# The seam between two transformer layers: which PSUM pool stays open, which engine rounds, and in which banks the row maxima stand

## The chip, the cores and the metric

The kernel runs on one core of one Trainium2 chip. The metric is the device time of the whole kernel in microseconds (us), the median of three runs. The core has five engines, each with its own queue in which instructions are taken in order: TensorE (PE, matmuls, its weight loads shown as PEld), VectorE (DVE), ScalarE (ACT), GpSimd (POOL) and SyncE (SP, which here issues most of the DMA transfers). Matmul results land in PSUM, eight banks of 512 fp32 words in each of 128 partitions; everything else on the chip stands in SBUF.

## The reference

The reference computes two layers of a diffusion backbone over 512 latent tokens and 256 context tokens, all with 1024 channels. Cut to what matters here:

```
for l in range(2):
    h   = rmsnorm(x) * (1 + scale) + shift          # "n1", modulated by the conditioning vector
    u   = h @ w_in                                  # one combined projection
    a   = glu -> depthwise conv(31) -> layernorm -> silu -> projection       # conv mixer
    b   = bidirectional mLSTM, 4 heads of 256 (gates: log_sigmoid, running sums and maxima), times o-gate
    c   = attention, 8 query heads and 2 key heads of 64, QK norm, axial rotary
    x  += gate * ((sigmoid(g_i) * (a, b, c)) @ w_out)
    x  += gate2 * ffn(modulated rmsnorm(x))         # gated, width-3 depthwise conv before the activation
```

Context tokens use the same weights with their own modulation, and read context tokens only. The output is the latent stream, so the second layer needs no context rows after its keys and values.

## The kernel before

**Layout.** Activations stand with channels on the partitions: eight tiles `xs[m]` of 128 channels by 768 positions, 512 latent (the segment X) and 256 context (XC). Layer 0 computes both, in PSUM tiles of 768 columns; layer 1 works on the latent positions, with the context only for keys and values.

**Precision.** Products are made from fp32 values that are split in a rounded high part and a low part. Every weight block of 128 x 128 thus gives three matmuls in `accumulate` (L717): high times high, and the two mixed products. The activations of a norm are `hh` and `hl`, the weights `wh` and `wl`.

**Weights.** All weights come through one stream in units of four blocks. SP loads a unit into `raw`; `Weights.split` lets ScalarE make `wh` (L215) and GpSimd `wl` (L217). In two kinds of stage the flag `W.shared` is set: where the merged mixers are projected, and in layer 0's last projection for the context half. There VectorE makes `wl` for odd units. A unit is split SPLITS units ahead of use.

**Order of the work.** TensorE's order is written out by hand. A `Filler` holds a queue of projections; `fill.step()` issues one k-step of the projection at the head and then a tick to all "chains", generators in which `yield n` means "go on after n ticks". Chains carry what VectorE, ScalarE and GpSimd do, and the small matmuls among it. `fill.settle()` ticks until all chains have ended, without further projection steps.

**PSUM.** Four banks are the small pools `sm` and `pv`, two buffers each. The other four are the pool `mm` for projections: `open_banks(l)` makes two buffers of 1024 words in layer 0, and four of 512 in layer 1. At the end of layer 0 `layer.close()` (L1752) closes the one and `open_banks(1)` (L783) opens the other; the new one can be written when the last reader of the old one is done.

**The boundary between the layers.** Layer 0's last projection, "down", runs once for the latent positions and once for the context positions, 256 columns wide, with 8 output tiles m. When tile m is complete, VectorE adds it to the residual stream (`residual`, L1619), ScalarE squares the result (`Norm.square`, L637), VectorE adds the square to a running sum (L639), and SP stores the tile. Beside the context half runs the chain `norm.apply` for the latent half of layer 1's first norm: for each of 8 k, VectorE multiplies by the reciprocal root (L679), ScalarE scales and shifts (L680), VectorE rounds to `hh` (L687), and VectorE, for k = 2 and 4 GpSimd, makes `hl` (L372). The context half of the norm follows as a chain in layer 1.

**First stage of a layer.** `opt["first"]` gives the order of the first projections: in layer 0 the gates and q, k, Q, K abreast ("G"), then v of head 0; in layer 1 "Q g K v". When the gate projection is complete, its evacuation starts the chain `mgates`: exponentials, a logarithm, two running scans and small differences on 36 rows, and at the end the matmuls L904 and L906 that spread the result. Between its parts stand ticks, `yield 5, 1, 2, 1, 2, 2, 2, 1, 3, 2`, 21 in all. All projections but the last are drained, then the chains are settled, then the last projection follows.

**Heads of the mLSTM.** `HEADS` and `HEADS1` (layer 1) give for each head the projections that fill TensorE ("c" conv, "o0 o1" the output gate, "q v" the next head's) and the positions, counted in steps, at which the mLSTM's own parts are issued: D (decays), S (scores, and the denominators' sums L1131 behind them), R (row sum of the denominators, matmul L584 in `normalise`, then transfers that spread it) and V (product with v). `score_gap` is the number of ticks between two score pairs. There are two groups, 0 and 1, in each head of layer 1.

**Attention.** `prepare(i)` finds the row maxima of head i: a matmul of each block of 128 queries with 512 keys into a `pv` bank (L1472), reduced by VectorE (L1473); the same with 256 context keys, two query blocks to a bank (L1479, L1481); then a transposition `rp` (L1489) in `pv`. Between them stand ticks. The attention products use `pv` too (L1565), read by L1573. Beside them run the gate projections for the merge in `mm`, evacuated by L369.

Of the kernel before, what the change touches and what calls it, by code (L numbers as in the profile page):

```python
# [17 lines left out]
D = 1024  # L18
# [33 lines left out]
HEADS1 = [["c o0 o1 q v", "2:S0 4:D1 16:R0 22:S1 39:R1 40:V0 61:V1 61:D*"]] * 3 +     [["c o0 o1 b b x0", "2:S0 4:D1 15:R0 21:S1 35:R1 38:V0 51:V1 51:s"]]  # L52
# [3 lines left out]
    score_gap=5, rows_gap=4, mask_gap=2, prep=2)  # L56
OPT = [dict(COMMON, partial=2, heads=HEADS, early=1, first_max=5, send_gap=2, norm_gap=8, first="G v",
# [3 lines left out]
       dict(COMMON, partial=3, heads=HEADS1, early=1, first_max=8, send_gap=3, norm_gap=11, first="Q g K v",  # L61
# [126 lines left out]
class Weights:  # L188


    def __init__(self, nc, dram, l, pool, more):
        self.next, self.shared, self.more = None, False, more
# [27 lines left out]
    def take(self, *specs):  # L220
# [4 lines left out]
        if j <= 1 < j + len(specs):  # L225
            self.split(u + SPLITS + 1)
# [61 lines left out]
def build(tc, A):  # L288
# [3 lines left out]
    with ExitStack() as es:  # L292
# [327 lines left out]
        class Norm:  # L620


            def __init__(self, l, nw, sc0, sh0, opt):
# [5 lines left out]
                self.hs = []  # L629

            def square(self, k, x, seg):
# [6 lines left out]
                if k < KC - 1:  # L638
                    dve.tensor_tensor(out=self.acc[:, o:o + n], in0=self.acc[:, o:o + n], in1=q[:, o:o + n], op=ALU.add)  # L639
# [35 lines left out]
            def raw_block(self, xs, seg, k, r=None):  # L675
                o, n, s = seg
                y = t3()[:, o:o + n]
                if r is not None:
                    dve.tensor_tensor(out=y, in0=xs[k][:, o:o + n], in1=r[:, 0:n], op=ALU.mult)  # L679
                act.activation(out=y, in_=xs[k][:, o:o + n] if r is None else y, func=AF.Identity,  # L680
                               scale=self.amul[:, k, s:s + 1], bias=mods[self.l][:, self.sh0 + k, s:s + 1])
                return y

            def block_parts(self, y, seg, k):
                o, n, s = seg
                hh, hl = self.hs[k]
                dve.tensor_copy(hh[:, o:o + n], y)  # L687
                lo_part(hl[:, o:o + n], y, hh[:, o:o + n], dve if k in self.opt["dve_lo"] else pool)
# [9 lines left out]
            def apply(self, xs, seg, n, each):  # L698
# [9 lines left out]
                for k in range(KC):  # L708
                    yield each
                    y, y0 = self.raw_block(xs, seg, k + 1, r) if k < KC - 1 else None, y  # L710
                    self.block_parts(y0, seg, k)
# [1059 lines left out]
```

## Time and profile before

| | |
|---|---|
| median of 3 runs | 3040.97 us (3040.7 to 3048.51) |
| profiled execution, its own time | 3040.4 us |
| span of the profiled execution | 3038.6 us |
| TensorE busy | 2827.8 us, 93% of the span |
| VectorE busy | 1817.7 us, 60% |
| ScalarE busy | 1156.8 us, 38% |
| GpSimd busy | 1146.6 us, 38% |

The span runs from the first to the last instruction that the profiler recorded; the execution's own time holds what lies around it too. Busy times of an engine are sums over its instructions, and overlap between engines. In the rows below, a wait "A <- B" is idle time of A's engine that ended when B's instruction gave its signal. The granted clock (PEclk) is the share of full speed that TensorE was given in a stretch; it has two levels, 1.2 and 2.4 GHz, so that 0.75 means half of the stretch at each.

### The profile page before, as it was taken

What the parts mean: (1) busy time and instruction counts of PE and PEld (TensorE: products, weight loads), DVE (VectorE), ACT (ScalarE), POOL (GpSimd) and SP (SyncE); (2) the same over time, 40 slices, a digit from 0 to 9 for tenths busy, and PEclk for the clock granted to TensorE, in tenths of its full rate; (3) what the DMA queues carried; (4) which work ended last, traced back from release to release, by engine and by line L of the source; (5) the groups of instructions that cost most, each with busy time, mean ns of one, the idle gap of its engine ahead of it and who ended that gap; (6) DMA issues with size and microseconds to landing.
All of it is one profiled execution on the core that took longest, in us unless ns stands there. A gap on an engine that the chain in (4) does not pass through costs nothing. (4 is left out here: it accounts for less than half of the span.)

```text
span 3038.6 us, 42068 instructions
## 1 busy us (share of the span) xinstructions
PE 2827.8 (93%) x15970; PEld 2381.7 (78%) x15970; DVE 1817.7 (60%) x2521; ACT 1156.8 (38%) x2122; POOL 1146.6 (38%) x931
## 2 busy tenths in 40 slices
PE   7999999899889998999999988999889889899999
PEld 4888888787667887888888867887767567778887
DVE  4376787825554336876765555777774763554444
ACT  5224334324345334322322253433444344443333
POOL 2233343224244334333333333333344345444444
PEclk9999999999999999999999999999999999999999
DMA  6454334221010242333333232333322112423333
GB/s 242 133 149 69 58 67 68 49 60 52 28 28 29 63 130 93 115 101 118 118 115 115 75 102 68 65 75 67 65 75 69 39 38 76 154 87 100 93 96 110
DMA packets 156681, 262.47 MB, mean 86 GB/s; under 512 B 17784, under 2 KB 37624, under 8 KB 156480
## 3 DMA queue, kind: packets, MB, share of 16 engines
q1 hardware_dynamic: 142560, 249.67, 28.0%
q10 hardware_dynamic: 13920, 10.12, 3.1%
q8 instruction: 126, 2.06, 0.3%
q14 instruction: 75, 0.61, 0.1%
HBM read 247.05 MB, written 5.46 MB: 83 GB/s over the span
## 5 line engine op out<-in xcount | busy, mean ns | idle before, releaser
L217 POOL TENSOR_TENSOR wl<-raw,wh 128x512 fp32r<-128x512 f32 x659 | 904.6, 1379 | 1507.6 <-ACT wh L215 1461.0
L717 PE MATMUL mm<-hh,wh 128*128 128x512 f32 (+1 forms) x2672 | 963.6, 361 | 17.0 <-DVE big L1619 7.1
L717 PE MATMUL mm<-hh,wl 128*128 128x512 f32 (+1 forms) x2672 | 949.1, 355 | 10.7 <-POOL wl L217 10.6
L717 PE MATMUL mm<-hl,wh 128*128 128x512 f32 (+1 forms) x2672 | 954.4, 357 | 2.1 <-POOL hl L372 1.2
L215 ACT ACTIVATE wh<-raw 128x512 fp32r<-128x512 f32 x662 | 411.2, 625 | 580.2 <-PE mm L717 358.4
L717 PEld LDWEIGHTS mm<-hh,wh 128*128 128x128 f32 x2672 | 512.4, 192 | 113.3 <-issue 29.6
L717 PEld LDWEIGHTS mm<-hh,wl 128*128 128x128 f32 x2672 | 510.4, 191 | 89.4 <-POOL wl L217 15.5
L717 PEld LDWEIGHTS mm<-hl,wh 128*128 128x128 f32 x2672 | 512.3, 192 | 71.4 <-POOL hl L372 1.8
L717 PE MATMUL mm<-C,wh 128*128 128x512 f32 (+1 forms) x1168 | 410.2, 351 | 0.3 <-DVE C L372 0.3
L717 PE MATMUL mm<-B,wh 128*128 128x512 f32 (+1 forms) x976 | 344.4, 353 | 24.4 <-DVE big L1619 11.8
L717 PE MATMUL mm<-B,wl 128*128 128x512 f32 (+1 forms) x976 | 342.5, 351 | 9.2 <-POOL wl L217 8.8
L993 DVE SCALAR_TENSOR_TENSOR AC<-G,par,AC 128x783 f32<-128x783 f32 (+1 forms) x240 | 261.1, 1088 | 3.6
L717 PEld LDWEIGHTS mm<-C,wh 128*128 128x128 f32 x1168 | 226.6, 194 | 28.3 <-DVE C L372 0.5
L717 PEld LDWEIGHTS mm<-B,wh 128*128 128x128 f32 x976 | 190.1, 195 | 53.7 <-ACT wh L215 14.5
L717 PEld LDWEIGHTS mm<-B,wl 128*128 128x128 f32 x976 | 189.4, 194 | 37.4 <-POOL wl L217 14.2
L1669 DVE SCALAR_TENSOR_TENSOR AC<-mm,par,AC 128x511 f32<-128x511 f32 (+1 forms) x132 | 86.7, 656 | 199.0 <-ACT AC L1667 199.0
L1619 DVE SCALAR_TENSOR_TENSOR big<-mm,mod,big 128x512 f32<-128x512 f32 (+1 forms) x144 | 91.1, 657 | 116.3 <-PE mm L717 116.1
L1667 ACT ACTIVATE AC<-mm,par 128x768 f32<-128x768 f32 (+1 forms) x88 | 77.4, 880 | 145.0 <-PE mm L717 144.8
L372 POOL TENSOR_TENSOR P<-t,P 128x512 fp32r<-128x512 f32 (+1 forms) x64 | 75.1, 1175 | 139.2 <-ACT t L1550 111.2
L527 DVE SCALAR_TENSOR_TENSOR P<-C,cs,P 128x512 f32<-128x512 f32 x112 | 116.5, 1072 | 0.9 <-DMA C<-aw 0.9
L1565 PE MATMUL pv<-P,B 128*128 128x512 f32 (+1 forms) x336 | 94.6, 387 | 12.1 <-DVE G L1573 5.2
L1097 ACT ACTIVATE C<-rb,bias 128x128 f32<-128x128 f32 x312 | 96.4, 390 | 21.4 <-DMA rb<-rows 11.2
(282 smaller groups left out, 3726.5 us busy)
## 6 DMA issues: line engine op xcount, KB each, us to landing
raw<-ws SPq DMA_DIRECT2D x662, 256.0 KB, 2.6
C<-aw SPq DMA_DIRECT2D x104, 256.0 KB, 3.0
big<-aw SPq DMA_DIRECT2D x64, 256.0 KB, 4.7
P<-ws SPq DMA_DIRECT2D x30, 256.0 KB, 2.9
big<-xt SPq DMA_DIRECT2D x16, 384.0 KB, 6.3
rb<-rows ACTq DMA_DIRECT2D x40, 128.0 KB, 4.2
den<-rd ACTq DMA_DIRECT2D x40, 64.0 KB, 6.3
den<-rd SPq DMA_DIRECT2D x40, 64.0 KB, 6.3
```

What stands on the lines that cost most here:

```text
L215: self.nc.scalar.activation(out=hi, in_=raw, func=AF.Copy)
L217: eng.tensor_tensor(out=lo, in0=raw, in1=hi.bitcast(F32), op=ALU.subtract)
L372: (eng or dve).tensor_tensor(out=out, in0=src, in1=hi.bitcast(F32), op=ALU.subtract)
L527: dve.scalar_tensor_tensor(out=a_, in0=r_, scalar=cs[:, k, q:q + 1], in1=a_, op0=ALU.mult, op1=ALU.add)
L717: pe.matmul(ps[:, o:o + n], w[w_], h[h_][:, so:so + n], start=(k == 0 and i == 0 and o % 512 == 0), stop=(k == n_k - 1 and i == 2), skip_g ...
L993: dve.scalar_tensor_tensor(out=a, in0=t[:, j:j + cw], scalar=par(l, "cw", w0 + j), in1=a, op0=ALU.mult, op1=ALU.add)
L1097: act.activation(out=t[:, off + x * 128:off + x * 128 + 128], in_=rb[:, c0:c0 + 128], func=AF.Exp, bias=bcol(dr, h, key, qb))
L1565: pe.matmul(o_[:, 0:n_q], vblock(b, a_)[:, 64 * v_:64 * v_ + 128], b_[:, 0:n_q], start=(ki == 0 and x == 0), stop=(last and x == 2))
L1619: dve.scalar_tensor_tensor(out=xs[m][:, o:o + n], in0=ps[:, po:po + n], scalar=gain[:, m, s:s + 1], in1=xs[m][:, o:o + n], op0=ALU.mult, o ...
L1667: act.activation(out=t[:, 0:tq], in_=ps[:, 0:tq], func=AF.Identity, scale=fw(1), bias=fb)
L1669: dve.scalar_tensor_tensor(out=t[:, o + 1:o + n], in0=ps[:, o:o + n - 1], scalar=fw(0), in1=t[:, o + 1:o + n], op0=ALU.mult, op1=ALU.add)
```

## The change

It has seven parts.

1. The pool of layer 0 is no longer closed at layer 0's end. It stays open through layer 1's first projections, and is exchanged for the four buffers of 512 just before the first head.
2. `Norm` has a form `fold`, used for layer 1's first norm. VectorE multiplies by the reciprocal root and by the scale in one instruction. For k = 0, 1, 3, 5, 6, 7 ScalarE adds the shift and rounds to `hh` in one, and VectorE makes `hl` as (y + shift) − hh in one. For k = 2 and 4 ScalarE adds the shift, VectorE casts and GpSimd makes `hl`. For the context half, the running sums of squares are added by GpSimd.
3. While `shared` is set, weights are split one unit further ahead, and the parts of odd units go to tiles of the pool AC (`room`).
4. The ticks of `mgates` become 6, 2, 3, 2, 3, 3, 3, 2, 2, 4, 3, 33 in all, in both layers; the transfer of the row values stands alone between two of them.
5. Layer 1's first stage becomes "Q g K o v": the first half of head 0's output gate moves there from head 0.
6. In layer 1's heads the positions of R, S, V shift by some steps, and `score_gap` goes from 5 to 4.
7. The maxima over a latent block's keys go to `mm` tiles: in layer 0 two query blocks x 512 keys or four x 256 to a buffer of 1024, in layer 1 as many to a tile as before. The context queries' maxima and `rp` stay in `pv`.

The diff, without the rows that pass `room` on:

```diff
-HEADS1 = [["c o0 o1 q v", "2:S0 4:D1 16:R0 22:S1 39:R1 40:V0 61:V1 61:D*"]] * 3 +     [["c o0 o1 b b x0", "2:S0 4:D1 15:R0 21:S1 35:R1 38:V0 51:V1 51:s"]]
+HEADS1 = [["c o1 q v", "2:S0 4:D1 18:R0 25:S1 41:R1 42:V0 60:V1 60:D*"]] + [["c o0 o1 q v", "2:S0 4:D1 18:R0 25:S1 41:R1 42:V0 61:V1 61:D*"]] * 2 +     [["c o0 o1 b b x0", "2:S0 4:D1 15:R0 21:S1 35:R1 38:V0 51:V1 51:s"]]
...
-    score_gap=5, rows_gap=4, mask_gap=2, prep=2)
+    rows_gap=4, mask_gap=2, prep=2)
...
-       dict(COMMON, partial=3, heads=HEADS1, early=1, first_max=8, send_gap=3, norm_gap=11, first="Q g K v",
+       dict(COMMON, partial=3, score_gap=4, heads=HEADS1, early=1, first_max=8, send_gap=3, norm_gap=11, first="Q g K o v",
...
-            hi = self.pool.tile([128, UNIT * 128], F32R, tag="wh", name=f"wh{self.l}_{u}")
-            lo = self.pool.tile([128, UNIT * 128], F32R, tag="wl", name=f"wl{self.l}_{u}")
+            if self.shared and u % 2:
+                hi, lo = self.room(), self.room()
+            else:
+                hi = self.pool.tile([128, UNIT * 128], F32R, tag="wh", name=f"wh{self.l}_{u}")
+                lo = self.pool.tile([128, UNIT * 128], F32R, tag="wl", name=f"wl{self.l}_{u}")
...
-            self.split(u + SPLITS + 1)
+            self.split(u + SPLITS + 1 + self.shared)
...
-                    dve.tensor_tensor(out=self.acc[:, o:o + n], in0=self.acc[:, o:o + n], in1=q[:, o:o + n], op=ALU.add)
+                    (pool if s and self.fold else dve).tensor_tensor(out=self.acc[:, o:o + n], in0=self.acc[:, o:o + n], in1=q[:, o:o + n], op=ALU.add)
...
             def raw_block(self, xs, seg, k, r=None):
                 o, n, s = seg
-                y = t3()[:, o:o + n]
-                if r is not None:
-                    dve.tensor_tensor(out=y, in0=xs[k][:, o:o + n], in1=r[:, 0:n], op=ALU.mult)
-                act.activation(out=y, in_=xs[k][:, o:o + n] if r is None else y, func=AF.Identity,
-                               scale=self.amul[:, k, s:s + 1], bias=mods[self.l][:, self.sh0 + k, s:s + 1])
+                y, shift = t3()[:, o:o + n], mods[self.l][:, self.sh0 + k, s:s + 1]
+                if r is None:
+                    act.activation(out=y, in_=xs[k][:, o:o + n], func=AF.Identity, scale=self.amul[:, k, s:s + 1], bias=shift)
+                else:
+                    dve.tensor_tensor(out=y, in0=xs[k][:, o:o + n], in1=r[:, 0:n], op=ALU.mult) if not self.fold else \
+                        dve.scalar_tensor_tensor(out=y, in0=xs[k][:, o:o + n], scalar=self.amul[:, k, s:s + 1], in1=r[:, 0:n],
+                                             op0=ALU.mult, op1=ALU.mult)
+                    if not self.fold:
+                        act.activation(out=y, in_=y, func=AF.Identity, scale=self.amul[:, k, s:s + 1], bias=shift)
+                    elif k not in self.opt["dve_lo"]:
+                        act.activation(out=y, in_=y, func=AF.Identity, bias=shift)
                 return y
 
-            def block_parts(self, y, seg, k):
+            def block_parts(self, y, seg, k, shifted=True):
                 o, n, s = seg
-                hh, hl = self.hs[k]
-                dve.tensor_copy(hh[:, o:o + n], y)
-                lo_part(hl[:, o:o + n], y, hh[:, o:o + n], dve if k in self.opt["dve_lo"] else pool)
+                hh, hl = [h[:, o:o + n] for h in self.hs[k]]
+                if shifted or k not in self.opt["dve_lo"]:
+                    dve.tensor_copy(hh, y)
+                    lo_part(hl, y, hh, dve if k in self.opt["dve_lo"] else pool)
+                else:
+                    shift = mods[self.l][:, self.sh0 + k, s:s + 1]
+                    act.activation(out=hh, in_=y, func=AF.Identity, bias=shift)
+                    dve.scalar_tensor_tensor(out=hl, in0=y, scalar=shift, in1=hh.bitcast(F32), op0=ALU.add, op1=ALU.subtract)
...
+        room = lambda: tac(UNIT * 128, F32R)
...
-            if l:
-                layer = open_banks(l)
...
-                yield 5
+                yield 6
...
                     dve.tensor_tensor(out=rr[P_, nat], in0=g[P_, sc], in1=ms[P_, sc], op=ALU.subtract)
+                yield 2
                 act.dma_start(out=rdram, in_=rr[R, :])
-                yield 1
+                yield 2
...
+                elif what == "o":
+                    fill.add(o_gate(0, 0))
...
             fill.drain()
+            if l:
+                layer.close()
+                layer = open_banks(l)
...
                     q0, nb = o // 128, n // 128
-                    if s == 0:
-                        for qb in range(q0, q0 + nb):
-                            ps = pv()
-                            pe.matmul(ps, q1[:, qb * 128:qb * 128 + 128], ks_[v_][:, 0:L], start=True, stop=True)
-                            dve.reduce_max(out=mx[:, qb:qb + 1], in_=ps, axis=AX.X)
-                            yield opt["prep"]
-                    m_ = mc if s == 0 else mx
-                    for qb in range(q0, q0 + nb, 2):
-                        ps = pv()
-                        for j in range(2):
-                            pe.matmul(ps[:, j * C:j * C + C], q1[:, (qb + j) * 128:(qb + j) * 128 + 128], ks_[v_][:, L:T],
-                                      start=(j == 0), stop=True, skip_group_check=True)
-                        dve.reduce_max(out=m_[:, qb:qb + 2], in_=ps.rearrange("p (j n) -> p j n", j=2), axis=AX.X)
-                        if qb + 2 < q0 + nb:
-                            yield opt["prep"]
+
+                    for to, keys_, per in ((mx, slice(0, L), banks[1] // L), (mc, slice(L, T), banks[1] // C)):
+                        if s:
+                            to, per = mx, 2
+                        if s and keys_.start == 0:
+                            continue
+                        nk = keys_.stop - keys_.start
+                        for qb in range(q0, q0 + nb, per):
+                            ps = mm(per * nk) if s == 0 else pv()
+                            for j in range(per):
+                                pe.matmul(ps[:, j * nk:j * nk + nk], q1[:, (qb + j) * 128:(qb + j) * 128 + 128],
+                                          ks_[v_][:, keys_], start=(j * nk % 512 == 0), stop=True, skip_group_check=True)
+                            dve.reduce_max(out=to[:, qb:qb + per], in_=ps[:, 0:per * nk].rearrange("p (j n) -> p j n", j=per),
+                                           axis=AX.X)
+                            if keys_.start == 0 or qb + per < q0 + nb:
...
-                    norm = Norm(l + 1, "n1", 8, 0, OPT[l + 1])
+                    norm = Norm(l + 1, "n1", 8, 0, OPT[l + 1], True)
...
-            layer.close()
+            if l:
+                layer.close()
```

`tac` gives a tile of the pool AC, which the mixers use. `lo_part` is a subtraction, L372.

## Rows read from the trace of the kernel before

**Rows 1.** Page, part 1: busy us (share of the span) and instructions of each engine.

```profile
PE 2827.8 (93%) x15970; PEld 2381.7 (78%) x15970; DVE 1817.7 (60%) x2521; ACT 1156.8 (38%) x2122; POOL 1146.6 (38%) x931
```

**Rows 2.** Windows: stretch and length in us, then the columns that the head names.

```profile
core 0: us, PE busy (x) PEld busy (x) DVE busy (x) ACT busy (x) POOL busy (x), PEclk, DMA share, GB/s
89.20:103.50 14.30, 11.18 (x47) 9.91 (x48) 6.08 (x22) 3.33 (x7) 3.27 (x3) 0.64 0.30 92
...
1135.20:1174.00 38.80, 29.29 (x189) 27.03 (x185) 29.88 (x45) 18.97 (x33) 15.54 (x12) 0.87 0.34 109
1754.80:1785.40 30.60, 15.85 (x121) 14.22 (x120) 21.96 (x39) 15.11 (x26) 9.82 (x8) 0.88 0.39 123
1807.50:1843.50 36.00, 27.39 (x155) 24.75 (x154) 22.19 (x41) 17.16 (x27) 9.01 (x9) 0.81 0.19 61
1850.00:2200.00 350.00, 325.27 (x1986) 284.75 (x1986) 258.80 (x378) 141.12 (x334) 131.78 (x117) 0.97 0.35 69
...
2750.00:2800.00 50.00, 49.94 (x221) 41.04 (x220) 23.83 (x29) 18.52 (x30) 24.02 (x19) 1.00 0.33 95
```

**Rows 3.** Waits of PE over the span: us in total, times, the longest.

```profile
PE mm L717 <- POOL wl L217: 20.2, 27, 2.6
...
PE sm L904 <- DVE t L889: 11.7, 2, 8.6
```

**Rows 4.** Waits of PE, 1754 to 1786.

```profile
PE mm L717 <- DVE big L1619: 14.3, 4, 7.1
```

**Rows 5.** Timeline, 1776 to 1787: start, length, instruction, idle time before and its releaser.

```profile
1781.01 0.47 DVE L1619 SCALAR_TENSOR_TENSOR big<-mm,mod,big 128x256 f32<-128x256 f32 x1
...
1784.78 0.48 DVE L1619 SCALAR_TENSOR_TENSOR big<-mm,mod,big 128x256 f32<-128x256 f32 x1
...
1785.40 0.77 PE L717 MATMUL mm<-hh,wh 128*128 128x512 f32 x1 [7.11 <-DVE big L1619]
```

**Rows 6.** Lines of DVE by form, 1754.8 to 1788: busy, mean ns, idle before.

```profile
L687 DVE CAST hh<-t 128x512 fp32r<-128x512 f32 x8 | 5.6, 700 | 0.0
L679 DVE TENSOR_TENSOR t<-big,sm 128x512 f32<-128x512 f32 x8 | 5.4, 680 | 0.0
L372 DVE TENSOR_TENSOR hl<-t,hh 128x512 fp32r<-128x512 f32 x6 | 4.2, 692 | 0.2
...
L639 DVE TENSOR_TENSOR rs<-rs,t 128x256 f32<-128x256 f32 x6 | 3.3, 548 | 3.1 <-ACT t L637 3.1
...
L1619 DVE SCALAR_TENSOR_TENSOR big<-mm,mod,big 128x512 f32<-128x512 f32 x1 | 0.8, 752 | 0.5 <-PE mm L717 0.5
```

**Rows 7.** Timeline of DVE and POOL, 1767 to 1773.

```profile
1766.83 0.42 DVE L687 CAST hh<-t 128x512 fp32r<-128x512 f32 x1
...
1769.53 1.29 POOL L217 TENSOR_TENSOR wl<-raw,wh 128x512 fp32r<-128x512 f32 x1 [6.19 <-ACT wh L215]
...
1769.85 1.25 DVE L687 CAST hh<-t 128x512 fp32r<-128x512 f32 x1
```

**Rows 8.** Timeline of DVE, 1854 to 1859, v of head 0.

```profile
1856.95 0.42 DVE L372 TENSOR_TENSOR C<-mm,C 128x256 fp32r<-128x256 f32 x1 [0.45 <-ACT C L366]
```

**Rows 9.** Waits of PE, 1850 to 2200, the heads of layer 1.

```profile
PE sm L584 <- DVE den L1131: 23.6, 8, 3.6
```

**Rows 10.** Waits of PE, 2350 to 2550, attention of layer 1.

```profile
PE pv L1472 <- DVE mx L1473: 14.7, 12, 5.3
PE pv L1489 <- DVE mx L1485: 3.1, 4, 0.9
```

**Rows 11.** Waits of PE, 750 to 1000, attention of layer 0.

```profile
PE pv L1472 <- DVE mx L1473: 9.3, 7, 6.6
PE pv L1565 <- DVE G L1573: 4.4, 2, 2.2
```

**Rows 12.** Lines of DVE by form, 700 to 1000.

```profile
L1473 DVE TENSOR_REDUCE mx<-pv 128x1 f32<-128x512 f32 x32 | 21.8, 685 | 8.5 <-PE pv L1472 8.4
```

**Rows 13.** Lines of POOL by form, 1754.8 to 1808.

```profile
L372 POOL TENSOR_TENSOR hl<-t,hh 128x256 fp32r<-128x256 f32 x2 | 1.5, 745 | 3.4 <-DVE hh L687 3.4
```

More of the change, by code (lines that the diff above doesn't have):

```diff
@@ L51 @@
 HEADS = [["c o0 o1 q v", "0:D1 2:S0 6:R0 9:S1 18:D2 22:V0 24:R1 26:S2 41:R2 44:V1 60:V2 60:D*"]] * 3 +     [["c o0 o1 b b x0", "0:D1 2:S0 6:R0 9:S1 18:D2 24:R1 26:S2 28:V0 40:R2 44:V1 52:s 56:V2"]]
-HEADS1 = [["c o0 o1 q v", "2:S0 4:D1 16:R0 22:S1 39:R1 40:V0 61:V1 61:D*"]] * 3 +     [["c o0 o1 b b x0", "2:S0 4:D1 15:R0 21:S1 35:R1 38:V0 51:V1 51:s"]]
+HEADS1 = [["c o1 q v", "2:S0 4:D1 18:R0 25:S1 41:R1 42:V0 60:V1 60:D*"]] + [["c o0 o1 q v", "2:S0 4:D1 18:R0 25:S1 41:R1 42:V0 61:V1 61:D*"]] * 2 +     [["c o0 o1 b b x0", "2:S0 4:D1 15:R0 21:S1 35:R1 38:V0 51:V1 51:s"]]
 COMMON = dict(
     gates=[(branch, m) for branch in (1, 0, 2) for m in range(KC)],
-    score_gap=5, rows_gap=4, mask_gap=2, prep=2)
-OPT = [dict(COMMON, partial=2, heads=HEADS, early=1, first_max=5, send_gap=2, norm_gap=8, first="G v",
+    rows_gap=4, mask_gap=2, prep=2)
+OPT = [dict(COMMON, partial=2, score_gap=5, heads=HEADS, early=1, first_max=5, send_gap=2, norm_gap=8, first="G v",
             fgroups=[4, 4, 4, 4, 2, 4], skew=2,
@@ L188, with __init__ @@
 class Weights:
-    def __init__(self, nc, dram, l, pool, more):
-        self.next, self.shared, self.more = None, False, more
+    def __init__(self, nc, dram, l, pool, more, room):
+        self.next, self.shared, self.more, self.room = None, False, more, room
         self.nc, self.dram, self.l, self.pool = nc, dram, l, pool
@@ L628, in __init__ @@
                 self.amul = None
-                self.hs = []
+                self.hs, self.fold = [], fold
             def square(self, k, x, seg):
@@ L710, in apply @@
                     y, y0 = self.raw_block(xs, seg, k + 1, r) if k < KC - 1 else None, y
-                    self.block_parts(y0, seg, k)
+                    self.block_parts(y0, seg, k, not self.fold)
         def accumulate(ps, w, h, k, n_k, sts, segs=None):
@@ L755, in build @@
         more = lambda u: alloc("P", PB, UNIT * 128)
-        W = Weights(nc, A["ws"], 0, wp, more)
+        room = lambda: tac(UNIT * 128, F32R)
+        W = Weights(nc, A["ws"], 0, wp, more, room)
         first = ada_first()
@@ L788, in build @@
             if wc:
-                W.next = Weights(nc, A["ws"], l + 1, wp, more)
+                W.next = Weights(nc, A["ws"], l + 1, wp, more, room)
             plans.append(W.blocks)
@@ L859, in mgates @@
                 dve.tensor_tensor(out=e[R, :], in0=e[R, :], in1=u[R, :], op=ALU.mult)
+                yield 3
+                dve.tensor_tensor(out=ln[R, :], in0=ln[R, :], in1=e[R, :], op=ALU.subtract)
                 yield 2
-                dve.tensor_tensor(out=ln[R, :], in0=ln[R, :], in1=e[R, :], op=ALU.subtract)
-                yield 1
                 for P_, nat, sc in dirs:
@@ L894, in mgates @@
                                       op1=ALU.mult)
-                yield 2
+                yield 3
                 for dr in range(2):
```

13 lines of the change are left out of this document (7 added, 6 removed).

## Prediction

> **What bounds the kernel now.** I read the page first for the busiest engine. TensorE is busy for 2827.8 us of the span [rows 1]: the work is nearly all matmuls, and the change neither adds nor removes one that costs anything. What can go is the 210.8 us in which it is idle (3038.6 − 2827.8), and the time in which it runs at half clock. Next I read the table of windows, over the stretches that the change touches [rows 2]. The last of its rows is how the kernel should look: in 50 us the engine is busy for 49.94, at a granted clock of 1.00, 221 matmuls of mostly 512 columns, so 0.226 us each and 0.113 us per 256 columns. The others are the places where it fails. At the boundary between the layers (1754.8 to 1785.4) TensorE is busy for half the time and the clock is 0.88. A clock of 0.88 means that a part of the stretch ran at 1.2 instead of 2.4 GHz. If all of it was work that full clock would halve, (1 − 0.88) × 30.6 = 3.7 us were lost that way; I use this product as an upper bound of what the clock can return in each window. Then the waits give the releaser: over the whole span POOL's low halves of the weights and the gate chain (L904) [rows 3], and by window the places below.
>
> **Boundary between the layers.** Its work is 32 blocks × 3 matmuls of 256 columns, 96 × 0.113 = 10.9 us, and it takes 30.6. Four waits on VectorE's residual add L1619 hold 14.3 us of it [rows 4]. The timeline shows what is late: the last two residuals start at 1781.01 and 1784.78, and layer 1's first matmul follows at 1785.40 [rows 5]. Nothing in that matmul needs the last residual, which belongs to the context half. It waits because the new PSUM pool takes the place of the closed one, whose last reader this residual is. VectorE's in-order queue is the bound: between residuals it does layer 1's norm [rows 6]. The change takes from this queue:
> - six square sums L639, 6 × 0.548 = 3.3 us;
> - six of the casts L687, which ScalarE now does in the instruction that it already had for the shift: between 6 × 0.42 (the short cast in [rows 7]) = 2.5 and 6 × 0.70 [rows 6] = 4.2 us.
>
> It adds to the remaining ones: eight multiplications L679 become an instruction with a scalar operand, and six low parts L372 too. No row shows these with their operands; the nearest is the 512-wide L1619 at 0.752 beside 0.680 and 0.692 [rows 6]. The lower bound is nothing, the upper 14 × 0.07 = 1.0 us; I take 1.0. So the queue gets 4.8 to 6.5 us shorter. With the old pool open, Q waits only for the buffer of the residual before the last, 1784.78 − 1781.01 = 3.8 us sooner. The sum is 8.6 to 10.3, with the clock up to 14; the loss left over is that the ScalarE pass is now between the multiply and the low part, and GpSimd's sums can come late. Cover for the last residual and for the context row sum is Q's own matmuls; without it the low end is 5. I take **−10** (−14 to −5).
>
> **The port.** In the timeline a cast of VectorE takes 1.25 us while a split of GpSimd runs from 1769.53 to 1770.82, and both end within 0.3 us; three microseconds earlier a cast of the same shape takes 0.42 [rows 7]. The Trainium skill, SBUF — State Buffer, section "Who interferes with whom", says why: the two engines share one port pair, a cast or a VectorE operation with two SBUF inputs excludes a GpSimd one that reads SBUF, and the second waits for the whole of the first. The trace agrees for the cast (1.25 against 0.42). By that rule the six sums do not leave the port when they go to GpSimd; that is a rival below.
>
> **Closing the pool later.** The pool is now exchanged after v of head 0. There TensorE goes on at once today, while v's copies still run: the last low part of v out of an `mm` buffer starts at 1856.95 and takes 0.42 [rows 8]. The conv matmul that shares a new bank must wait for that: nothing if the first banks taken are long free, about 4 us if it waits for all four copies and a queue. I take **+1.5** (0 to +4).
>
> **Gate chain, both layers.** The gate matmuls L904 wait 11.7 us in two places, 8.6 (layer 1) and 3.1 (layer 0) [rows 3]. They stand in TensorE's order at a place set by the chain's ticks, 21 before, 33 after (one tick per projection step). Layer 0: the 12 further ticks are cut short where the chains are settled, at v's start; about 8 more steps then lie ahead of the gate matmuls, each 3 × (0.226 + 0.113) = 1.0 us for 768 columns, so the wait of 3.1 goes, and with it the 0.64 clock over 14.3 us, up to 0.36 × 14.3 = 5.1 [rows 2]. I take **−7** (−8 to −3). What is late next is the bias that head 0's first D step reads; it now has the same steps fewer of cover, hence the low end. Layer 1: `o` is moved ahead of the settling of the chains, which puts 8 steps × 3 × 0.226 = 5.4 us of matmuls under the chain's 8.6. But the chain's own instructions also stand later in VectorE's and ScalarE's queues, behind the copies of K; I estimate half the cover lost, 2.7, from the same 5.4. The clock there is 0.81 over 36 us, up to 6.8 [rows 2]; a shorter hole returns little of it. I take **−3** (−9 to 0). The transfer of the row values on ScalarE's queue gets a tick of its own; its data are then ready, so nothing queued behind it (ScalarE's copies) waits: in the term.
>
> **Head positions in layer 1.** In 1850 to 2200 the row matmuls L584 wait for the denominators' result L1131 eight times, 23.6 us [rows 9]: twice in each head. In heads 0 to 2 the first of the two gets 4 more projection steps of 3 × 0.226 = 0.68 us: 2 from its own position, 2 from the smaller `score_gap`. In head 3 it gets the 2. At a mean wait of 23.6 / 8 = 2.95, that covers 2.7 × 3 + 1.4 = 9.5. The second of each head moves with what it waits for and stays. Head 0 loses 8 steps (its `o0`) ahead of V0 and R1, which takes some back. The clock is 0.97 over 350 us, so it can return little more [rows 2]. I take **−7** (−12 to −3).
>
> **Maxima in the projections' banks.** Layer 1: the four-buffer pool `mm` takes the tiles that the two `pv` buffers hold today, so TensorE can run two reductions further ahead; 12 waits of L1472 hold 14.7 us, four of L1489 (which stays) 3.1 [rows 10]. Those waits are on one queue, VectorE's, where other work stands ahead of the reductions; more buffers move a wait only if the queue catches up. Half of 14.7, less what the projections that share the banks wait: **−6** (0 to −20, both lines gone, 14.7 + 3.1, and 2 of clock). Layer 0: the same waits hold 9.3 us, and attention's first use of `pv` after the reads L1573 4.4 more [rows 11]; these shrink. Against it, the two 1024-wide buffers serve projections and maxima now: a max tile takes the buffer just left by a projection or the other way round, so the next one waits for an evacuation or for a reduction of 1024 columns, 2 × 0.685 = 1.37 us [rows 12]. Tile counts fall from 4 to 2 and 2 to 1, so most allocations have half the waits. I take **−2** (−18, all gone and the clock with them, to +20, below).
>
> **Merged stages, weights one unit ahead.** TensorE waits 20.2 us, 27 times, for POOL's low parts [rows 3], much of it in the two stages where the weights are split by two engines: in layer 0's the clock is 0.87 over 38.8 us [rows 2]. One unit more ahead is 12 matmuls × 0.113 = 1.4 us of cover per wait where the columns are 256 and 2.7 where 512, and the added tiles stand in the otherwise idle room of the mixers. GpSimd's rate is not changed, so where it is the bound nothing is gained: **−5** (−12 to 0).
>
> **Sum.** −10 + 1.5 − 7 − 3 − 7 − 6 − 2 − 5 = −38.5. The profiled execution took 3040.4 us, 1.8 more than its span, and the median of the runs is 3041.0; so 3040.4 − 38.5 = 3001.9, **3002 us**.
>
> **Rivals.**
> - Waits come back: VectorE's queue is in order, and what no longer stalls at one place stands at the next (R1 instead of R0, L1489 instead of L1472). Then the terms for heads, maxima and merged stages give a third, 7 of 20, and the gates half: −10 + 1.5 − 5 − 7 = −20.5, **3020**. For it: of 210 us idle, the waits with a name are spread over many lines. Against it: boundary and gate chain are holes with one cause.
> - The port: the sums moved to GpSimd still exclude VectorE, 6 × 0.745 = 4.5 us, priced by GpSimd's operation of the same width [rows 13], against the 3.3 saved. The boundary then gives −5, the sum −33.5, **3007**. For it: the cast at 1.25 us. That is what the rule of the Trainium skill's SBUF — State Buffer, cited above, would do here. Against it: residuals and multiplications read PSUM, the sums come early, and GpSimd is busy 9.8 of 30.6 us [rows 2].
> - The change does nothing that can be seen: the new shared banks cost what the rest gains (about 40 allocations × 0.9 us). **3040**.
> - Slower: layer 0's two wide buffers. Some 24 tiles of maxima and 20 projections alternate on them; if each waits for the other's reader, 44 × 1.37 = 60 us new, with the rest (−36.5): **3064**. It decides from 36.5 / 44 = 0.83 us each on. For it: before, maxima and projections never met. Against it: a projection's step of 24 matmuls is longer than a reduction, so a buffer is mostly free when its turn comes.
>
> **Chances.** Forecast 0.55, waits come back 0.20, port 0.09, nothing 0.08, slower 0.08. About 0.3%, 9 us, is what can be told from no change; the first three lie beyond it: faster 0.84, same 0.08, slower 0.08. All low ends together are −93, 54.5 below the sum; they will not come together, and with some 45% of it, 24 us, the range begins at 2978. Up to 3028 the port and the waits that come back are in, and little more than the last two cases is left out.
>
> **What would show it.** In the trace after: layer 1's first projection within 2 us of the residual before the last, and no L1619 wait over 4 us; L904 without a wait in layer 0 and 3 to 6 us in layer 1; L584 under 16 us in the heads; L1472 on `mm` under 10 us in layer 1; fewer waits on `wl`. Wrong if the maxima show waits on `mm` by L369's or the reductions' readers in layer 0, or if VectorE's queue at the boundary is not shorter because its operations take longer.

## The result, and the profile after

The changed kernel takes **3000.74 us** (median of 4, 2999.28 to 3002.32), beside 3044.74 for the kernel before (4 runs); the ratio is 0.9852, with a 95% interval of 0.9828 to 0.9876. The fourth run of the kernel before, at 3052.82 us, is what moved its median up from 3040.97. The forecast was 3002. By the medians the gain is 44.0 us; the profiled execution's span went from 3038.6 to 2999.0 us, 39.6 less, where the prediction's sum was 38.5. That agreement is luck: most of the terms are wrong one by one, and they cancel. The page of the changed kernel, part 1:

```profile
PE 2817.0 (94%) x15970; PEld 2376.6 (79%) x15970; DVE 1812.0 (60%) x2476; ACT 1152.6 (38%) x2118; POOL 1155.0 (39%) x937
```

To see where the time went, both traces were cut at the same work: both kernels issue the same 12,672 matmuls with weights, so the n-th one is a mark (the edges of a stretch move the numbers by up to 0.4 us). The first column gives the times of the marks in the kernel before; the others are the length of each stretch minus that of before. The predicted terms stand beside them.

| stretch of before | what runs | predicted | changed | maxima alone | all but maxima |
|---|---|---|---|---|---|
| 40 to 150 | gate chain, layer 0 | −7 | −1.6 | −1.0 | −2.0 |
| 150 to 661 | heads of layer 0 (code unchanged) | 0 | +4.5 | +2.9 | +1.1 |
| 661 to 985 | up to the end of the maxima, layer 0 | −2 | −21.0 | −22.1 | +2.7 |
| 1104 to 1210 | merged stage, layer 0 | part of −5 | −5.1 | +1.0 | −4.5 |
| 1705 to 1786 | boundary, up to Q's start | −10 | −5.6 | −1.5 | −5.6 |
| 1786 to 2190 | first stage and heads, layer 1 | +1.5 − 3 − 7 | +6.2 | −0.6 | +4.2 |
| 2341 to 2573 | maxima, layer 1 | −6 | −16.0 | −16.3 | +0.2 |
| 2598 to 2699 | merged stage, layer 1 | part of −5 | −2.8 | +0.1 | −2.5 |

Stretches that are left out differ by 0.7 us at most. The two stages of maxima give 37 of the 39.6 us. The windows of the changed kernel, over the stretches that answer to [rows 2] (gates of layer 0, boundary, gates of layer 1, heads) and over both stages of maxima (the second and the last row):

```profile
core 0: us, PE busy (x) PEld busy (x) DVE busy (x) ACT busy (x) POOL busy (x), PEclk, DMA share, GB/s
85.00:110.00 25.00, 21.13 (x130) 18.61 (x129) 13.94 (x31) 6.28 (x11) 4.31 (x4) 0.86 0.32 99
740.00:970.00 230.00, 214.21 (x1175) 172.89 (x1174) 141.67 (x176) 119.87 (x225) 100.26 (x85) 0.98 0.11 34
1731.70:1760.20 28.50, 17.91 (x126) 15.99 (x125) 16.54 (x27) 13.78 (x25) 14.75 (x15) 0.83 0.43 135
1780.00:1820.00 40.00, 34.43 (x191) 30.85 (x191) 23.18 (x40) 18.90 (x27) 15.81 (x12) 0.87 0.24 69
1826.00:2180.00 354.00, 322.56 (x1969) 280.56 (x1968) 258.44 (x378) 139.10 (x330) 130.73 (x115) 0.96 0.34 67
2330.00:2515.00 185.00, 170.34 (x741) 129.30 (x742) 137.76 (x188) 87.50 (x158) 84.45 (x64) 0.98 0.16 46
```

In layer 0's maxima TensorE is now busy for 214 of 230 us at a clock of 0.98. The heads of layer 1 have the same clock as before within 0.01 and more idle time. The waits of TensorE over the whole span, changed kernel, to be read beside [rows 3] and [rows 9 to 11] (L588 is L584 of before, L919 L904, L1499 the maxima's matmul, L1640 L1619):

```profile
PE sm L588 <- DVE den L1146: 27.3, 13, 4.4
PE mm L732 <- POOL wl L221: 20.7, 25, 2.0
PE mm L732 <- DVE big L1640: 17.3, 12, 3.4
...
PE mm L1499 <- DVE mx L1501: 9.7, 12, 4.0
PE sm L919 <- DVE t L904: 9.4, 2, 5.6
```

The weights' low parts cost TensorE as much as before (20.7 beside 20.2), although the part meant for them works: they moved, as the heads will show.

### The profile page after: what moved, and what is told of

The parts are those of the page before. It is cut to its first block, busy times and chain, and to the rows that moved or that the text cites. A ratio compares the mean times of both kernels' runs of the same rounds, so it can differ in the third digit from the quotient of the medians.

```text
span 2999.0 us, 41978 instructions
## 1 busy us (share of the span) xinstructions
PE 2817.0 (94%) x15970; PEld 2376.6 (79%) x15970; DVE 1812.0 (60%) x2476; ACT 1152.6 (38%) x2118; POOL 1155.0 (39%) x937
## 5 line engine op out<-in xcount | busy, mean ns | idle before, releaser
L221 POOL TENSOR_TENSOR wl<-raw,wh 128x512 fp32r<-128x512 f32 x659 | 910.4, 1388 | 1470.0 <-ACT wh L219 1401.3
L732 PE MATMUL mm<-hh,wh 128*128 128x512 f32 (+1 forms) x2664 | 962.7, 361 | 18.5 <-DVE big L1640 3.8
L732 PE MATMUL mm<-C,wh 128*128 128x512 f32 (+1 forms) x1068 | 376.9, 353 | 0.3 <-DVE C L376 0.3
L732 PE MATMUL mm<-B,wh 128*128 128x512 f32 (+1 forms) x876 | 311.0, 355 | 19.0 <-DVE big L1640 11.6
L732 PE MATMUL mm<-B,wl 128*128 128x512 f32 (+1 forms) x876 | 308.3, 352 | 5.2 <-POOL wl L221 5.1
L732 PEld LDWEIGHTS mm<-C,wh 128*128 128x128 f32 x1068 | 202.7, 190 | 28.2 <-DVE C L376 0.5
L732 PEld LDWEIGHTS mm<-B,wh 128*128 128x128 f32 x876 | 166.6, 190 | 47.2 <-issue 12.6
L732 PEld LDWEIGHTS mm<-B,wl 128*128 128x128 f32 x876 | 166.3, 190 | 30.7 <-POOL wl L221 8.3
L1640 DVE SCALAR_TENSOR_TENSOR big<-mm,mod,big 128x512 f32<-128x512 f32 (+1 forms) x144 | 90.9, 656 | 114.1 <-PE mm L732 113.9
L376 POOL TENSOR_TENSOR P<-t,P 128x512 fp32r<-128x512 f32 (+1 forms) x64 | 75.2, 1176 | 113.4 <-ACT t L1571 87.5
L1197 PE MATMUL pv<-P,C 128*128 128x256 f32 x624 | 96.5, 293 | 5.6 <-DVE P L376 2.9
```

What stands on the lines that cost most here:

```text
L221: eng.tensor_tensor(out=lo, in0=raw, in1=hi.bitcast(F32), op=ALU.subtract)
L376: (eng or dve).tensor_tensor(out=out, in0=src, in1=hi.bitcast(F32), op=ALU.subtract)
L732: pe.matmul(ps[:, o:o + n], w[w_], h[h_][:, so:so + n], start=(k == 0 and i == 0 and o % 512 == 0), stop=(k == n_k - 1 and i == 2), skip_g ...
L1197: pe.matmul(ps[:, dd * 256:dd * 256 + 256], v_[key // 3][:, vo:vo + 128], b_, start=(ki == 0 and i == 0 and dd == 0), stop=(ki == len(part ...
L1640: dve.scalar_tensor_tensor(out=xs[m][:, o:o + n], in0=ps[:, po:po + n], scalar=gain[:, m, s:s + 1], in1=xs[m][:, o:o + n], op0=ALU.mult, o ...
```

## The experiments

All were timed beside the kernel before. Two kernels that differ by 3 us are not told apart by such medians: the intervals of the ratios reach 3 to 7 us to either side, and every small edit of the changed kernel below has a ratio within the changed kernel's own interval or at its edge. So small edits are judged by waits and stretches of the traces, one trace for each kernel.

**The maxima alone, and all but the maxima.** To the kernel before, or out of the changed one:

```diff
-                            ps = pv()        # maxima over a latent block
+                            ps = mm(per * nk) if s == 0 else pv()
```

> The kernel before with one part alone: the maxima over latent query blocks go to the projections' banks, in both layers. Theory A (read from the two traces, the maxima carry the gain): layer 0's attention gets about 21 us shorter and layer 1's about 16, 3004 us in all. Theory B (the terms of the prediction): 2 and 6 us, 3033. Rival C (the gain needs the other parts, because they shift what stands in VectorE's queue): some 20 us, 3020.

> The changed kernel with the maxima alone put back to the two small banks. Theory A: 33 to 37 us are lost, about 3036. Theory B: 8 us are lost, about 3009, since the boundary, the gates, the heads and the merged stages would carry 30.

Measured: alone 3005.78 us (ratio 0.9874, 0.9858 to 0.9891), all but 3037.72 (0.9976, 0.9965 to 0.9987). Theory A holds in both directions: the maxima carry the gain, by themselves and in each stretch. The prediction's terms, 8 and 30 us, are refuted. In layer 1 the tiles' width, their number and the ticks are as before, so there the bigger pool alone gives the 16 us.

**Narrow tiles.** The kernel before with maxima in `mm`, but in layer 0 tiles of 512 columns:

```diff
-  ((mx, slice(0, L), banks[1] // L), (mc, slice(L, T), banks[1] // C))
+  ((mx, slice(0, L), 1), (mc, slice(L, T), 2))
```

> The kernel before with the maxima in the projections' banks, but in layer 0 with tiles of 512 columns as before (six tiles and reductions for each head's latent block instead of three), one tile to a buffer of 1024. Theory A (what counted was the two small banks, shared with the attention products and the transposition): layer 0's attention still gains most of 23 us, 3004 to 3010. Rival B (what counted were the wider tiles: fewer reductions, 12 ticks instead of 18): layer 0's attention gains under 8 us, 3020 to 3027. Rival C (two buffers with twice as many tiles make the projections wait, the slower rival of the prediction): over 3030.

Measured: 3036.25 us (0.9968, 0.9958 to 0.9977). Layer 0's maxima became 6.2 us longer than before, up to 985; layer 1's, which are the same as in the kernel with the maxima alone, 16.3 shorter. So Rival C has the time right and A is refuted; B was right that nothing is gained without the wider tiles, and wrong in the size. But C's reason is not what the waits show: the maxima's own matmuls wait for the reductions, 13.1 us, and the projections for them only 1.4. Waits of TensorE in 740 to 1000 of this kernel (L1479 is the maxima's matmul, L1566 attention's):

```profile
PE mm L1479 <- DVE mx L1481: 13.1, 12, 4.2
PE pv L1566 <- DVE G L1574: 4.4, 2, 2.2
PE pv L1479 <- DVE G L1574: 4.2, 2, 2.3
```

and in 740 to 970 of the changed one:

```profile
PE pv L1510 <- DVE mx L1501: 5.8, 2, 5.1
PE mm L1499 <- DVE mx L1501: 4.8, 10, 1.4
```

With narrow tiles the wait of [rows 11] only changes its bank, from 9.3 on `pv` to 13.1 on `mm`, and the waits for L1573's reads (now L1574) stay to the tenth. With wide tiles both go. These waits for L1573 are more than the one row of [rows 11]. The same view of the kernel before has six further lines of waits for a `pv` buffer, 12.0 us together, among them:

```profile
PE pv L1479 <- DVE G L1573: 4.2, 2, 2.3
PE pv L1565 <- DVE B L1573: 2.2, 1, 2.2
PE pv L1479 <- DVE B L1573: 1.9, 1, 1.9
```

So what the two small banks cost in layer 0 was 25.7 us by the rows, not 9.3 and 4.4. The reduction's price, lines of VectorE by form, changed kernel, 690 to 985:

```profile
L1501 DVE TENSOR_REDUCE mx<-mm 128x2 f32<-128x1024 f32 x16 | 19.5, 1221 | 7.8 <-PE mm L1499 7.8
L1501 DVE TENSOR_REDUCE mc<-mm 128x4 f32<-128x1024 f32 x8 | 9.7, 1214 | 4.7 <-PE mm L1499 4.7
```

A reduction of 1024 columns takes 1.22 us, less than 2 × 0.685 [rows 12], and there are 24 hand-overs of a buffer instead of 48. Narrow tiles also keep 18 ticks in a head's chain where wide ones have 12, so that the context maxima can come later and meet attention's use of `pv`; no run shows that this is the reason. Width and ticks were changed together, and which of them frees `pv` is open.

**Ticks of layer 0's gate chain as before.**

```diff
-                yield 6          # and the ten after it
+                yield 5 if l == 0 else 6
```

> The changed kernel with the gate chain's ticks of before in layer 0 alone. Theory A (traces: more ticks delay the chain itself as much as the matmuls that need it, the wait only moves from 89 to 98 us): same time within 2 us, a wait of about 3 us at 89 and none at 98. Theory B (the prediction): the ticks give 7 us, so 3008.

Measured: 2998.47 us, not told apart from 3000.74. The gate matmuls (L920 here, L919 in the changed kernel) wait 3.1 us, and in the changed kernel 3.9, at 98 instead of 89 us. Waits of TensorE, 80 to 110, first this kernel, then the changed one:

```profile
PE sm L920 <- DVE t L905: 3.1, 1, 3.1
```

and:

```profile
PE sm L919 <- DVE t L904: 3.9, 1, 3.9
```

This is Theory A. The timeline of the changed kernel shows why the ticks buy nothing:

```profile
86.36 0.81 ACT L370 ACTIVATE B<-mm 128x768 fp32r<-128x768 f32 x1 [4.39 <-PE mm L732]
87.20 0.96 DVE L376 TENSOR_TENSOR B<-mm,B 128x768 fp32r<-128x768 f32 x1 [4.15 <-ACT B L370]
...
96.80 0.96 DVE L376 TENSOR_TENSOR B<-mm,B 128x768 fp32r<-128x768 f32 x1 [2.47 <-ACT B L370]
...
97.67 1.50 DVE L892 TENSOR_TENSOR C<-C,C 32x512 f32<-32x512 f32 x1
```

The chain's next step (L892) now stands in VectorE's queue behind the low part of a projection (L376), which waits for that projection by way of ScalarE's copy (L370); VectorE stands idle for 4.15 and 2.47 us there. The chain is late by as much as its consumer.

**Head positions of layer 1 as before.**

```diff
-... 18:R0 25:S1 41:R1 42:V0 ...   score_gap=4
+... 16:R0 22:S1 39:R1 40:V0 ...   score_gap=5
```

> The changed kernel with layer 1's head positions and its score gap of before (head 0 still without its first output gate). Theory A (the traces: the heads of layer 1 became 6 us longer, with new waits on the weights' low parts): 3 to 6 us faster than the changed kernel, about 2996, and the waits on low parts in the heads gone. Theory B (the prediction): the positions give 7 us, so about 3008, and L584's waits back at 23 us. Rival C: positions do not matter, 3000 within 2, waits only change their names.

Measured: 2997.43 us; the stretch 1786 to 2190 is +3.3 instead of +6.2. The median is 3.3 us lower, which alone is no proof; with the stretch it speaks for Theory A, and Theory B is refuted: the positions are no gain. Waits of TensorE in the heads, the changed kernel (1826 to 2180), then this one (1823 to 2177):

```profile
PE sm L588 <- DVE den L1146: 18.5, 8, 3.6
PE mm L732 <- POOL wl L221: 7.1, 6, 2.0
```

and:

```profile
PE sm L588 <- DVE den L1146: 23.7, 10, 3.9
```

The cover works, 5.2 us where 7 were taken, and 7.1 come back as waits on the weights' low parts, none of which this kernel shows. GpSimd's timeline, changed kernel, 1860 to 1875:

```profile
1860.57 1.28 POOL L221 TENSOR_TENSOR wl<-raw,wh 128x512 fp32r<-128x512 f32 x1 [0.55 <-ACT wh L219]
1867.85 0.85 POOL L1174 TENSOR_TENSOR C<-C 128x256 f32<-128x256 f32 x1 [6.00 <-DVE C L1172]
...
1872.21 2.93 POOL L221 TENSOR_TENSOR wl<-raw,wh 128x512 fp32r<-128x512 f32 x2
```

GpSimd stands idle for 6 us at the head's sum L1174, which waits for VectorE's product, while two splits (L221) are queued behind it and behind the sums after it. The first split's high part was ready when ScalarE ended it at 1866.96, so 0.9 us of the idle time and all of the sums stand ahead of a split that could have run; it starts 5.3 us later, and TensorE waits 2.0 us for it.

**The boundary: pool closed early, no fold, sums on VectorE.**

```diff
# pool closed early
+            layer.close()                # at the end of each layer
# no fold
-   norm = Norm(l + 1, "n1", 8, 0, OPT[l + 1], True)
+   norm = Norm(l + 1, "n1", 8, 0, OPT[l + 1])
# sums on VectorE
-   (pool if s and self.fold else dve).tensor_tensor(out=self.acc...
+   dve.tensor_tensor(out=self.acc...
```

> The changed kernel with the PSUM pools exchanged at the end of layer 0 again, as before. Theory A (traces of the changed kernel: layer 1's first matmul follows the residual before the last at once, and that residual ends 3.8 us before the last; the exchange after v costs a wait of 2.15): about 1.7 us slower, 3002. Theory B (the prediction: 3.8 less 1.5, and clock for the longer hole): 2.3 to 6 us slower, 3003 to 3007. Rival C: the hole at the boundary is set by VectorE's queue alone, and only the wait of 2.15 goes: 2 us faster.

> The changed kernel with the norm between the layers as before (shift, cast and low part in separate instructions, sums of squares on VectorE). Theory A (traces: the changed VectorE works 5.4 us less at the boundary but now waits for ScalarE's rounding three times, 1.4 us each): 1 to 3 us slower, 3002. Theory B (the prediction: the queue is 4.8 to 6.5 us shorter, and that is what the boundary gains): 5 to 6 us slower, 3006. Rival C: nothing, the pool alone made the gain: same within 1.

> The changed kernel with the sums of squares of the context half back on VectorE, everything else as changed. Theory A: VectorE has idle time between its residuals now, so the sums fit in: same within 1 us. Theory B (the prediction's term): 6 x 0.548 = 3.3 us slower. Rival C (the port: the sums on GpSimd hold VectorE off as long as they take): up to 1 us faster.

Measured: 2997.35, 2996.34 and 2998.01 us; none is slower than the changed kernel's 3000.74. In the traces the stretch 1705 to 1786 is −1.8 with the early close (3.8 us lost, as both theories say), −5.2 without the fold, −3.6 with the sums on VectorE (0.5 us more idle time of TensorE). The exchange after v costs a wait of 2.15 us in the changed kernel and none with the early close, so by the waits the late close is worth 3.8 − 2.15 = 1.7 (Theory A). It is not shown in the time: the stretch after the boundary, 1786 to 2190, is 3.1 us shorter with the early close, which leaves 0.7, and the median is 3.4 us the other way. The fold is worth 0.5 us of idle time here, and nothing in the median. The timeline of the changed kernel, to be read beside [rows 5 to 7]:

```profile
1743.37 1.27 POOL L221 TENSOR_TENSOR wl<-raw,wh 128x512 fp32r<-128x512 f32 x1
...
1743.70 1.49 DVE L703 SCALAR_TENSOR_TENSOR hl<-t,mod,hh 128x512 fp32r<-128x512 f32 x1 [0.31 <-ACT hh L702]
...
1749.58 0.75 DVE L703 SCALAR_TENSOR_TENSOR hl<-t,mod,hh 128x512 fp32r<-128x512 f32 x1 [1.46 <-ACT hh L702]
...
1753.58 0.75 DVE L686 SCALAR_TENSOR_TENSOR t<-big,amul,sm 128x512 f32<-128x512 f32 x1 [1.47 <-POOL hl L376]
...
1755.73 0.75 DVE L703 SCALAR_TENSOR_TENSOR hl<-t,mod,hh 128x512 fp32r<-128x512 f32 x1 [1.41 <-ACT hh L702]
...
1757.82 0.47 DVE L1640 SCALAR_TENSOR_TENSOR big<-mm,mod,big 128x256 f32<-128x256 f32 x1
1758.44 0.77 PE L732 MATMUL mm<-hh,wh 128*128 128x512 f32 x1 [3.11 <-DVE big L1640]
...
1761.65 0.47 DVE L1640 SCALAR_TENSOR_TENSOR big<-mm,mod,big 128x256 f32<-128x256 f32 x1
```

Q now follows the residual before the last, as predicted. But VectorE, which works 16.5 us here instead of 22.0 [rows 2], waits for ScalarE's rounding before the low part, and before a multiplication for GpSimd's low part (1.47 and once more 1.00 us): part of what it no longer does it waits for.

**Weights no further ahead, and only where the mixers are merged.**

```diff
# no AC tiles, no further ahead
-   self.split(u + SPLITS + 1 + self.shared)
+   self.split(u + SPLITS + 1)
# only in the merged stages: a flag, cleared in layer 0's last projection
-   W.shared = seg == segs[1]
+   W.shared, W.ahead = seg == segs[1], False
```

> The changed kernel without the tiles of the pool AC for odd weight units, and with the weights split no further ahead than before. Theory A (traces: the stages with merged mixers are 4.5 to 5.1 and 2.3 to 2.8 us shorter in every kernel with this part, 0 to 1 longer in the one without): 7 us slower, 3008, with the waits on low parts in these stages back at 7.6 and 6.5. Theory B (the prediction): 5 us slower, 3006. Rival C (GpSimd's rate is the bound): same.

> The changed kernel, with the AC tiles and the unit further ahead only where the mixers are merged, not in layer 0's last projection. Theory A (the boundary is 9.5 us shorter without this part and 5.6 with it, because the low part that VectorE makes earlier stands ahead of residuals and of the reciprocal that the norm needs): about 3.9 us faster, 2997, and no wait over 3.5 us at the boundary but that for Q. Rival B (the 3.9 is the scatter of half-clock stretches): same within 1.5.

Measured: 3003.76 without the part, 2990.57 us with it in the merged stages alone (ratio to before 0.9826, 0.9806 to 0.9845, beside 0.9828 to 0.9876 for the changed kernel: its four runs, 2990.36 to 2996.36, lie below the changed kernel's four, but the intervals of the ratios overlap). Waits of TensorE in layer 0's merged stage, the changed kernel (1087 to 1189), then the one without the part (1088 to 1196):

```profile
PE mm L732 <- DVE big L1640: 4.3, 4, 2.8
PE mm L732 <- POOL wl L221: 3.3, 4, 1.0
```

and:

```profile
PE mm L732 <- POOL wl L221: 8.6, 9, 2.6
PE mm L732 <- ACT wh L219: 3.0, 3, 1.6
```

The two merged stages gain 6.1 and 2.9 us by it. In the boundary it costs: TensorE's idle time from 1705 to 1786 is 14.6 to 14.7 us in the changed kernel and the three others whose edit is elsewhere (all but the maxima, the ticks, the head positions), and 10.6 to 10.8 in these two and in the kernel named best below. So the part is worth 5 us net in the traces, and 3.0 by the medians; both theories for the kernel without it (3008, 3006) left out the boundary. The timeline of the changed kernel, 1734 to 1740, shows one of the waits:

```profile
1734.69 1.36 DVE L221 TENSOR_TENSOR AC<-raw,AC 128x512 fp32r<-128x512 f32 x1 [1.80 <-ACT AC L219]
...
1736.60 0.36 PE L732 MATMUL mm<-B,wh 128*128 128x256 f32 x1 [0.87 <-DVE amul L668]
```

VectorE makes a low part early (L221), ahead of a residual, and TensorE waits for what stands behind it. Of the 10.2 us between the medians 4 are thus explained, by idle time (2.3 by the length of the stretch); the heads and the FFN of layer 0 have the same code and are 4.2 and 3.0 us shorter in this profile, for a reason given in the last section.

**Together, with and without the fold.** The kernel named best has the part in the merged stages, and the ticks of layer 0 and the head positions of before; the other is the same without the fold:

```diff
-   norm = Norm(l + 1, "n1", 8, 0, OPT[l + 1], True)
+   norm = Norm(l + 1, "n1", 8, 0, OPT[l + 1])
```

> The parts that the stretches of the runs speak for together: the changed kernel with the AC tiles only where the mixers are merged, the gate chain's ticks of before in layer 0, and layer 1's head positions and score gap of before. Theory A (the three add up): 3.9 + 2 + 3, 2992. Rival B (each was scatter): 2998 to 3001.

> The kernel of the run named best with the norm between the layers as before (no fold, sums of squares on VectorE). Theory A (with the early low part of the weights gone from the boundary, the shorter VectorE queue counts there): 3 to 4 us slower than best, 2996. Rival B (VectorE's wait for ScalarE's rounding eats it, as in the run without the fold): same within 1.5, or faster by 1.

Measured: 2993.66 and 3000.04 us (ratios to before 0.9831, 0.9816 to 0.9847, and 0.9847, 0.9828 to 0.9867). The median of best lies nearer to Theory A's 2992 than to Rival B's range, but it is no faster than the one edit above, which at 2990.57 us has the lowest median of all kernels run; and from 1786 to 2190 best is at +4.5 beside that one's +4.4. So it is not shown that ticks and positions add anything. With the early low parts gone, the fold seems to be worth something: the boundary is −9.5 with it and −3.8 without. Waits of TensorE there, first with (1730 to 1756), then without (1730 to 1762):

```profile
PE mm L732 <- DVE big L1641: 6.1, 4, 3.0
```

and:

```profile
PE mm L732 <- DVE big L1641: 8.0, 4, 3.7
```

1.9 of the 5.7 us are waits. The rest goes with a longer time at 1.2 GHz in that stretch (18.5 us beside 4.6), which cannot be put down to the fold for certain.

## Why the prediction was right in the sum and wrong in its terms

Of the prediction's signs, four came: Q within 2 us of the residual before the last, no residual wait over 4 us (3.4), the gate matmuls of layer 1 at 5.6 us, and the maxima's waits on `mm` in layer 1 at 4.8. Three did not: the gate matmuls of layer 0 still wait (3.9), the heads' row matmuls wait 18.5 us and not under 16, and the waits on `wl` are 20.7 beside 20.2. One of its signs of being wrong came too, waits of the maxima on `mm` in layer 0, though without the loss that it was to announce. Term by term:

- **Maxima in layer 0**, −2: measured −21.0. Two steps failed. The first is "so the next one waits for an evacuation or for a reduction of 1024 columns": narrow tiles show such waits (13.1 us), but at the width of the change they are at most 1.4 us each, so the term charged far too much against the gain. The second is the gain itself: it was read from two rows, 9.3 and 4.4, with "these shrink"; six more lines of the same view, 12.0 us, were left out, and none of the 25.7 is left; with it went half of the time at 1.2 GHz (20.5 to 10.2 us in that stage). What is left on `pv` is chiefly a wait of the transposition for its input, 5.8. The slower rival fails at the first step: it needed 0.83 us for each of 44 allocations; the maxima's ten waits on `mm` in 740 to 970 sum to 4.8, and with all others on `mm` there it is 8.8, or 0.2 each.
- **Maxima in layer 1**, −6: measured −16.0. The mechanism was right, the term mis-sized: not half of L1472's waits goes but two thirds, 14.7 [rows 10] to the 4.8 of the row below (waits of TensorE, changed kernel, 2330 to 2515), and the time at 1.2 GHz falls from 17.1 to 10.2 us, which is 3.4 us of time.

```profile
PE mm L1499 <- DVE mx L1501: 4.8, 2, 4.0
```

- **Boundary**, −10: −5.6, of which 1.5 come also in the kernels with the maxima alone, whose boundary is not edited. With the same fold and pool but without the weights' part there, three kernels measure −7.9 to −9.5. The step that failed is "much of it in the two stages where the weights are split by two engines": layer 0's last projection is a third place with `shared` set, and there the part was priced at nothing and costs 4 us of idle time. VectorE's queue did get 5.5 us shorter, as priced, but part of that came back as "the loss left over", the waits for ScalarE's rounding.
- **Closing later**, +1.5: a wait of 2.15, near what was taken.
- **Gate chain**, −7 in layer 0: −0.6 beside the kernel with the maxima alone. "so the wait of 3.1 goes" failed: VectorE's queue is in order, so the chain was moved along with its consumer. In layer 1 the wait fell from 8.6 to 5.6, as taken (5.9); no run takes the added ticks and the moved `o` apart there.
- **Heads**, −7: the cover came near what was taken (−5.2), the rival "waits come back" took more than it (7.1 on low parts). With the exchange's 2.15, the gate chain's 3 less and 3 us of small new waits (2.0 of them L588's for L1207), idle time from 1786 to 2190 went from 32.9 to 36.6 us, and the time at 1.2 GHz from 39.7 to 45.7, half of which is lost: 3.7 + 3.0 make the stretch's +6.2 but for 0.5. So this rival was right for the heads, and wrong for the maxima, to which it gave a third of 8 us.
- **Merged stages**, −5: −7.9 there, right in kind, and less the boundary's 4 about −4.
- **The port**: the longer operations are there (1.49 and 1.77 us for L703 beside 0.75 in the trace; GpSimd splits from 1743.37 to 1744.64), as the rule in the Trainium skill's SBUF — State Buffer, "Who interferes with whom", would have it. As a rival for the time it fails: with the sums back on VectorE the boundary is 2.0 us longer, 0.5 of it idle time, and the median 2.7 us lower, which is no sign that the sums on GpSimd cost anything.

## What to carry to other kernels

Add up the waits of all users of a small buffer pool before you price a way out of it: the two longest rows said 9.3 and 4.4, all of them 25.7, and 21 us went, half of the time at 1.2 GHz with them. In layer 1 a bigger pool did it by itself; in layer 0 it did nothing without wider tiles and fewer ticks. Giving a chain more ticks moves its steps behind whatever its engines issue in between, so before adding slack, read what the in-order queues of its own engines hold there. And an agreement of the total proves no term: cut both traces at the same work and compare stretch by stretch.

## What the runs showed that was not expected

Stretches whose code no edit touches differ between the traces, some by the clock alone. From 1210 to 1705 (FFN of layer 0, same code) TensorE's idle time is 8.1 us in the kernel before, the changed one, the one without the fold and the one with the weights' part in the merged stages alone; the time at 1.2 GHz is 6.8, 6.8, 0 and 0 us, and the stretch lasts 495.1, 495.2, 491.6 and 492.2. In the heads of layer 0 (120 to 661) the idle time lies between 21.7 and 25.2 us and the time at 1.2 GHz between 6.8 and 20.5, over all traces. And the boundary of the two kernels that leave it as before (the maxima alone, wide and narrow) has 16.3 to 16.4 us of idle time beside 18.8. So 3 to 5 us of any two of these kernels' difference can come from a place that neither edits.
